# Two gate rows of a modulation: summed by 32-column ones products and spread by DMA instead of by full-width ones products

## The chip, the core and the metric

The kernel runs on 1 core of one Trainium2 chip. The metric is the device time of one execution in microseconds (us); the median of several executions is compared. Engines are named as the profile names them: PE (TensorE), PEld (its weight load), DVE (VectorE), ACT (ScalarE), POOL (GpSimd), SP (SyncE, which here only issues DMAs).

## The reference, cut to what matters

Two transformer blocks on 256 rows of width 1024, all in f32. In the first block a conditioning vector `c` gives six rows of 1024 numbers, two of which are the gates:

```python
mod = jax.nn.silu(c) @ w_ada[l] + b_ada[l]
sh1, sc1, gt1, sh2, sc2, gt2 = jnp.split(mod[:, None, :], 6, axis=-1)
h = modulate(rmsnorm(x, g_norm1[l]), sh1, sc1)        # h * (1 + scale) + shift
...
x_new = x + gt1 * o                                    # o: attention and retention, through w_out
x_new = x_new + gt2 * conv_ffn(modulate(rmsnorm(x_new, g_norm2[l]), sh2, sc2),
                               w_up[l], conv_w[l], conv_b[l], w_down[l])
```

`gt1` and `gt2` multiply all 256 rows, so on the chip each must stand on all 128 partitions, 1024 columns wide. The second block (windowed attention, a gated recurrence, cross attention, a gated feed-forward) does not use the modulation.

## The kernel before, in words

Every large product is made of f32 matrices that are split in a high and a low part (`split_from`, L159, and `Weights.unit`, L217): ACT casts the high part (L223, or L230 with a gain), DVE subtracts to get the low part (L226, L231), and PE adds three products (`mm3`, L180, matmuls at L186). Weights come in 512 KB pieces into five `raw` buffers (L199), loaded by SP's queue (L211, L213). So a piece goes DMA, ACT, DVE, PE, and its `raw` buffer is free for SP's next load when ACT and DVE have read it.

The order of instructions on each engine is not written out: a scheduler behind the tile pools sets it from the program, each engine then works strictly in that order, and buffers of a pool go round. Pools that matter here: PSUM `tr` (2 buffers, L110) and `acc` (4), SBUF `s4` (128x1024, 9 buffers, L293) and `s1k` (128x256, 4 buffers, L295). In the traces `s` stands for a tile of the pool s1, `s4` tiles among them.

The modulation rows of groups 2 to 5 (gt1, sh2, sc2, gt2) are not made on PE alone. `tick` (L517) loads one 128x1024 piece of `w_ada` and DVE adds `silu(c)` times it to an accumulator of its group (L526, L529). With the eighth piece of a group `ada_done` (L496) is called: the accumulator has to be summed over its 128 partitions, which a product with a matrix of ones does. For the gates the full 128-column ones matrix leaves the sum on all 128 partitions at once (L502), in two halves of 512 columns, and DVE adds each half from PSUM to the bias row that already stands on all partitions (L504). For shift and scale only 32 columns of ones are used, four times 256 columns side by side in one PSUM tile (L507, L508), then `ada_fm` (L337) turns the rows.

Ticks fall into these loops: one per unit in the loop over the first 544 columns of `w_in` (L589 to L599), so group 2 is complete at its end; three per unit in strand D (L601), two in E and eight in F (L854, L855), so group 5 ends in the interleaved part that `WEAVE` (L30) writes out, beside attention (`mla_half`, L711) and retention (`retention`, L765). Right behind the loop at L589 stand the query part (L614 to L623), the key part (L639 to L653) with its transposes (L168), the query projection (`w_uq`, L660 to L683) with the rotation (`rope32`, L625; its last step is L636), and a copy inside SBUF by two DMAs from SP (L657). The first user of gt1 is `seg1` (L920), the first of gt2 is `seg2` (L1320), both far behind.

Of the kernel before, what the change touches and what calls it, by code (L numbers as in the profile page):

```python
# [14 lines left out]
ALU = mybir.AluOpType  # L15
# [3 lines left out]
P = 128  # L19
# [70 lines left out]
def _body(nc, tc, A, out, es):  # L90
# [18 lines left out]
    def tr_tile():  # L109
        return ps.tile([P, 512], F32, tag="tr", name="tr", bufs=2)  # L110
# [20 lines left out]
    ones = cp.tile([P, P], F32, name="ones")  # L131
# [156 lines left out]
    with ExitStack() as e1:  # L288
# [4 lines left out]
        S4 = lambda shape=(P, 1024), dt=F32: s.tile(list(shape), dt, tag="s4", name="s4", bufs=9)  # L293
# [11 lines left out]
        for b in range(2):  # L305
            c = slice(b * 512, (b + 1) * 512)
# [25 lines left out]
        def ada_rows(acc):  # L332
            rows = S1()
            nc.scalar.copy(rows, acc[:, 0:256])
            return rows

        def ada_fm(acc, bias, dst, ns=1):  # L337
            rows = ada_rows(acc)
            t = tr_tile()
            for b in range(2):  # L340
                nc.tensor.transpose(t[:, b * P:(b + 1) * P], rows[:, b * P:(b + 1) * P], ident)
            tv = t[:, 0:256].rearrange("p (b q n) -> p n q b", b=2, q=4)
            for i in range(ns):
                nc.vector.tensor_tensor(out=dst[:, 8 * i:8 * i + 8].rearrange("p (q b) -> p q b", b=2), in0=tv[:, i, :, :],
                                        in1=FM(bias).rearrange("p (q b) -> p q b", b=2), op=ALU.add)

        def scale_gain(dst, sc, gname):
            nc.vector.scalar_tensor_tensor(out=dst, in0=sc, scalar=1.0, in1=FM(gname), op0=ALU.add, op1=ALU.mult)
# [145 lines left out]
        bc_row(gt2, "b_gt2")  # L494

        def ada_done(g, acc):  # L496
            if g in (2, 5):
                dst = gt1 if g == 2 else gt2
                for i in range(2):
                    t = tr_tile()  # L500
                    ac = slice(i * 512, (i + 1) * 512)
                    nc.tensor.matmul(t, lhsT=ones, rhs=acc[:, ac], start=True, stop=True)  # L502
                    d = dst[:, i * 512:(i + 1) * 512]
                    nc.vector.tensor_tensor(out=d, in0=d, in1=t, op=ALU.add)  # L504
            else:
                t = tr_tile()
                for q in range(4):  # L507
                    nc.tensor.matmul(t[32 * q:32 * q + 32, 0:256], lhsT=ones[:, 0:32],  # L508
                                     rhs=acc[:, q * 256:(q + 1) * 256], start=True, stop=True)
                ada_fm(t, "b_sh2" if g == 3 else "b_sc2", B2 if g == 3 else A2)  # L510
            if g == 4:
                scale_gain(A2, A2, "g_norm2")
# [4 lines left out]
        def tick(n=1):  # L517
            for _ in range(n):
                if not ada_queue:
                    return  # L520
                g, k = ada_queue.pop(0)
                raw = W().raw()
                nc.sync.dma_start(raw, A["w_ada"][k * P:(k + 1) * P, g * 1024:(g + 1) * 1024])
                if k == 0:
                    ada_cur[g] = S4()
                    nc.vector.tensor_scalar(out=ada_cur[g], in0=raw, scalar1=silc[:, k, 0:1], scalar2=None,  # L526
                                            op0=ALU.mult)
                else:
                    nc.vector.scalar_tensor_tensor(out=ada_cur[g], in0=raw, scalar=silc[:, k, 0:1],  # L529
                                                   in1=ada_cur[g], op0=ALU.mult, op1=ALU.add)  # L530
                if k == 7:
                    ada_done(g, ada_cur[g])
# [871 lines left out]
    for g in range(1, 6):  # L1404
        nb = 4 if g < 5 else 2
        sg = G4()
        for part, mk, us in ((0, tr_tile, ones_w2["gate"][g]), (1, at_tile, ones_w2["up"][g])):
# [3 lines left out]
            for i in range(nb // 2):  # L1411
                c = slice(i * 512, (i + 1) * 512)
                if part == 0:
                    nc.vector.tensor_tensor(out=sg[:, c].rearrange("p (j n) -> p j n", j=2),
                                            in0=accs[i].rearrange("p (j n) -> p j n", j=2),
                                            in1=rbc.unsqueeze(1).broadcast_to([P, 2, T]), op=ALU.mult)
# [99 lines left out]
```

## Time and profile before

| | before |
|---|---|
| median of 3 runs | 854.78 us (853.59 to 857.85) |
| span of the profiled execution | 852.4 us, 12981 instructions |
| PE busy | 822.0 us (96%) |
| DVE busy | 575.9 us (68%) |
| ACT busy | 464.1 us (54%) |
| mean granted TensorE clock | 0.996 of full speed |
| DMA | 154.22 MB, mean 181 GB/s |

The span runs from the first to the last instruction of the profiled execution. A device time of that one execution by itself is not among the numbers; the median of the runs is 2.4 us above the span, and that difference stands for what lies around it.

A row of the timeline gives the start, the duration of one group, the engine, the line, the operation, output<-inputs, the shape and the count; in square brackets stands the idle time of that engine before it and what ended it. [...] "To landing" is the time from a DMA's issue to its last byte with its completion.

### The profile page before, as it was taken

The numbers are of one execution on the slowest core, as the hardware profiler recorded it, in microseconds if no ns is written. First come the engines' busy times: TensorE is split into PE (matmuls) and PEld (weight loads), VectorE is DVE, ScalarE is ACT, GpSimd is POOL, SyncE is SP. The second block draws the span as 40 slices with busy tenths as digits, with TensorE's granted clock in tenths as the row PEclk, the third lists the DMA queues.
The fourth block names the chain that finished last, engine by engine and source line by source line (L and its number), as shares of the span: only waits on it lengthen the run. The fifth ranks groups of instructions, "written<-read, shape, count | busy, mean of one in ns | idle before, by whom it ended". The sixth has DMA issues, their size and how long they took to land.

```text
span 852.4 us, 12981 instructions
## 1 busy us (share of the span) xinstructions
PE 822.0 (96%) x4978; PEld 689.9 (81%) x4978; DVE 575.9 (68%) x881; ACT 464.1 (54%) x749; POOL 53.0 (6%) x91
## 2 busy tenths in 40 slices
PE   6999989999999999999999999999999999999996
PEld 5767976666787898998997877777888899998995
DVE  4339778995787697667577767776847855655642
ACT  6739264234566675555455757665626845554631
POOL 1100020110010000000002200101001100000000
PEclk9999999999999999999999999999999999999999
DMA  8898787863155566666664543443624676666511
GB/s 287 306 316 276 225 257 245 286 228 119 50 161 170 180 219 194 177 191 182 183 188 148 166 144 112 130 141 124 194 78 126 191 227 186 186 186 185 174 50 50
DMA packets 65150, 154.22 MB, mean 181 GB/s; under 512 B 5184, under 2 KB 10816, under 8 KB 65088
## 3 DMA queue, kind: packets, MB, share of 16 engines
q1 hardware_dynamic: 65088, 153.39, 57.6%
q8 instruction: 39, 0.64, 0.3%
q14 instruction: 23, 0.19, 0.1%
HBM read 151.80 MB, written 1.05 MB: 179 GB/s over the span
## 4 chain that ended last, share of the span: by engine, by line
PE 66%; ACT 4%; DVE 3%; issue 1%; POOL 1%; DVEq 0%; POOLq 0%; ACTq 0%
PE acc L186 32%; PE tr L256 12%; PE at L256 12%; PE tr L168 1%; PE at L1280 1%; PE at L1258 1%; PE tr L1199 1%; ACT xh L223 1%; DVE xl L226 1%; ACT junk L144 1%; PE at L1149 1%; PE at L1151 1%; PE tr L742 0%; PE at L771 0%; PE at L788 0%
## 5 line engine op out<-in xcount | busy, mean ns | idle before, releaser
L223 ACT CAST wh<-raw 128x1024 fp32r<-128x1024 f32 (+1 forms) x90 | 91.2, 1015 | 105.9 <-PE acc L186 28.1
L226 DVE TENSOR_TENSOR wl<-raw,wh 128x1024 fp32r<-128x1024 f32 (+1 forms) x87 | 102.3, 1177 | 49.1 <-ACT wh L223 48.1
L226 DVE TENSOR_TENSOR xl<-raw,xh 128x1024 fp32r<-128x1024 f32 x68 | 84.4, 1245 | 43.9 <-ACT xh L223 43.6
L186 PE MATMUL acc<-wh,xTh 128*128 128x512 f32 (+2 forms) x272 | 100.4, 395 | 1.7 <-ACT wh L223 1.4
L223 ACT CAST xh<-raw 128x1024 fp32r<-128x1024 f32 x68 | 71.0, 1049 | 55.9 <-PE tr L256 24.6
L186 PE MATMUL acc<-wl,xTh 128*128 128x512 f32 (+2 forms) x272 | 97.3, 383 | 0.5 <-DVE wl L226 0.5
L186 PE MATMUL acc<-wh,xTl 128*128 128x512 f32 (+2 forms) x272 | 97.5, 383 | 0.0
L231 DVE SCALAR_TENSOR_TENSOR wl<-raw,fm,wh 128x512 fp32r<-128x512 f32 (+3 forms) x96 | 67.3, 744 | 44.4 <-ACT wh L230 43.8
L230 ACT ACTIVATE wh<-raw,fm 128x512 fp32r<-128x512 f32 (+3 forms) x96 | 63.8, 713 | 38.2 <-issue 16.7
L186 PEld LDWEIGHTS acc<-wh,xTh 128*128 128x128 f32 x272 | 50.4, 189 | 13.6 <-issue 2.4
L186 PEld LDWEIGHTS acc<-wl,xTh 128*128 128x128 f32 x272 | 50.5, 189 | 11.7 <-issue 2.3
L186 PEld LDWEIGHTS acc<-wh,xTl 128*128 128x128 f32 x272 | 50.5, 189 | 9.7 <-issue 1.0
L186 PE MATMUL acc<-xh,xTl 128*128 128x512 f32 x144 | 53.5, 397 | 0.0
L186 PE MATMUL acc<-xl,xTh 128*128 128x512 f32 x144 | 53.3, 396 | 0.2 <-DVE xl L226 0.2
L186 PE MATMUL acc<-xh,xTh 128*128 128x512 f32 x144 | 53.2, 397 | 0.0
L186 PE MATMUL acc<-xh,g 128*128 128x512 f32 x160 | 45.6, 397 | 0.0
L231 DVE SCALAR_TENSOR_TENSOR xl<-raw,fm,xh 128x512 fp32r<-128x512 f32 (+1 forms) x44 | 33.3, 796 | 17.8 <-ACT xh L230 17.7
L230 ACT ACTIVATE xh<-raw,fm 128x512 fp32r<-128x512 f32 (+1 forms) x44 | 31.2, 757 | 22.4 <-issue 12.9
L529 DVE SCALAR_TENSOR_TENSOR s<-raw,silc,s 128x1024 f32<-128x1024 f32 x28 | 39.0, 1393 | 6.2 <-DMA raw<-in_w_ada_dram 6.1
L186 PE MATMUL acc<-wh,g 128*128 128x512 f32 x128 | 37.1, 397 | 0.0
L186 PEld LDWEIGHTS acc<-xh,g 128*128 128x128 f32 x160 | 29.7, 189 | 6.7
L186 PEld LDWEIGHTS acc<-xl,xTh 128*128 128x128 f32 x144 | 26.7, 188 | 6.4 <-DVE xl L226 1.1
(373 smaller groups left out, 1745.1 us busy)
## 6 DMA issues: line engine op xcount, KB each, us to landing
raw<-in_w_up_dram SPq DMA_DIRECT2D x66, 512.0 KB, 3.8
raw<-in_w_ada_dram SPq DMA_DIRECT2D x48, 512.0 KB, 5.5
raw<-in_w_down_dram SPq DMA_DIRECT2D x44, 512.0 KB, 3.6
raw<-in_w_in_dram SPq DMA_DIRECT2D x38, 512.0 KB, 3.9
raw<-in_w_gate_dram SPq DMA_DIRECT2D x22, 512.0 KB, 4.1
raw<-in_w_out_dram SPq DMA_DIRECT2D x16, 512.0 KB, 3.6
raw<-in_wk_x_dram SPq DMA_DIRECT2D x8, 512.0 KB, 6.7
raw<-in_wv_x_dram SPq DMA_DIRECT2D x8, 512.0 KB, 5.7
```

The lines of the kernel that those rows point to most:

```text
L144: nc.scalar.activation(junk[:, 0:a.shape[-1]], a, AF.Square, scale=n ** -0.5, accum_out=ss)
L168: nc.tensor.transpose(t[:, j * P:(j + 1) * P], src[:, (b + j) * P:(b + j + 1) * P], ident)
L186: nc.tensor.matmul(accs[i], lhsT=xl if f == 2 else xh, rhs=wl[i] if f == 1 else wh[i], start=first and f == 0, stop=last and f == 2)
L223: nc.scalar.copy(wh[:, 0:n], raw[:, 0:n])
L226: eng.tensor_tensor(out=wl[:, 0:n], in0=raw[:, 0:n], in1=wh[:, 0:n].bitcast(F32), op=ALU.subtract)
L230: nc.scalar.activation(wh[:, s], raw[:, s], AF.Copy, scale=gains[k])
L231: nc.vector.scalar_tensor_tensor(out=wl[:, s], in0=raw[:, s], scalar=gains[k], in1=wh[:, s].bitcast(F32), op0=ALU.mult, op1=ALU.subtract)
L256: nc.tensor.matmul(accs[b // 2][:, (b % 2) * T:(b % 2 + 1) * T], lhsT=wt[:, o:o + P], rhs=xt[:, k, :], start=k == 0 and fl == 0 and b % 2 ...
L529: nc.vector.scalar_tensor_tensor(out=ada_cur[g], in0=raw, scalar=silc[:, k, 0:1], in1=ada_cur[g], op0=ALU.mult, op1=ALU.add)
L1149: nc.tensor.matmul(o[cs, hs], lhsT=ATs[cs, cols], rhs=ih[cs, hs], start=True, stop=cg == 0)
L1151: nc.tensor.matmul(o[cs, hs], lhsT=qi[:, cols], rhs=Sst[cg - 1][:, hs], start=False, stop=True)
L1199: nc.tensor.matmul(sc[:, j * nk:(j + 1) * nk], lhsT=qTs[pr_, hd * P:(hd + 1) * P], rhs=kTs[pr_, 0:nk], start=True, stop=True)
```

## The change

All four groups are now summed by the 32-column products, which leave column block q of the sum on partitions 32q to 32q+31. For the gates ACT copies them from PSUM to an `s1k` tile (`ada_rows`, L332), and four DMAs on ACT's own queue each read one row of 256 numbers (1 KB) from partition 0, 32, 64 or 96 and write it to all 128 partitions of a new `s4` tile (128 KB each). One DVE instruction of 128x1024 adds that tile to the bias row.

```diff
         def ada_done(g, acc):
+            t = tr_tile()
+            for q in range(4):
+                nc.tensor.matmul(t[32 * q:32 * q + 32, 0:256], lhsT=ones[:, 0:32],
+                                 rhs=acc[:, q * 256:(q + 1) * 256], start=True, stop=True)
             if g in (2, 5):
+                gt = S4()
                 dst = gt1 if g == 2 else gt2
-                for i in range(2):
-                    t = tr_tile()
-                    ac = slice(i * 512, (i + 1) * 512)
-                    nc.tensor.matmul(t, lhsT=ones, rhs=acc[:, ac], start=True, stop=True)
-                    d = dst[:, i * 512:(i + 1) * 512]
-                    nc.vector.tensor_tensor(out=d, in0=d, in1=t, op=ALU.add)
+                rows = ada_rows(t)
+                for q in range(4):
+                    c = slice(q * 256, (q + 1) * 256)
+                    nc.scalar.dma_start(gt[:, c], rows[32 * q:32 * q + 1, :].unsqueeze(1).broadcast_to([1, P, 256]))
+                nc.vector.tensor_tensor(out=dst, in0=dst, in1=gt, op=ALU.add)
             else:
-                t = tr_tile()
-                for q in range(4):
-                    nc.tensor.matmul(t[32 * q:32 * q + 32, 0:256], lhsT=ones[:, 0:32],
-                                     rhs=acc[:, q * 256:(q + 1) * 256], start=True, stop=True)
                 ada_fm(t, "b_sh2" if g == 3 else "b_sc2", B2 if g == 3 else A2)
```

The number of lines stays the same; in the changed kernel the products are L499, the DMAs L507 and the DVE addition L508.

The scheduler also places other instructions anew. In the rows below, `waits` lists the counters an instruction waits on: an engine's name, or DMAHW for the completion counters of DMAs (a number after the underscore only belongs to the name).

**Place 1** is the end of the loop at L589, where group 2 (gt1) is completed. On ACT before, between the two `w_uq` casts (L230) and the cast of strand D's first weight piece (L223), the query copies (L616) and sums of squares (L144) stand:

```order
L230 ACTIVATE wh<-raw,fm 128x768
L616 COPY s1k<-acc 128x256
L144 ACTIVATE junk,ss_1177<-acc 128x256
L230 ACTIVATE wh<-raw,fm 128x768
L616 COPY s1k<-acc 128x256
L144 ACTIVATE junk,ss_1189<-acc 128x256
L223 CAST wh<-raw 128x1024
```

On ACT with the change:

```order
L230 ACTIVATE wh<-raw,fm 128x768 x2
L223 CAST wh<-raw 128x1024
L334 COPY s1k<-tr 128x256
L616 COPY s1k<-acc 128x256
L507 DMA s_1168<-s1k 128x1x256 x4
L144 ACTIVATE junk,ss_1184<-acc 128x256
L160 CAST s_1176<-tr 128x2x128
L616 COPY s1k<-acc 128x256
```

The cast L223 has moved ahead of both query copies; the gate's copy and its four DMAs stand behind the first of them.

On DVE at the same place before, with the two gate additions (L504) and the query part's subtractions (L161) behind them:

```order
L504 TENSOR_TENSOR bc<-bc,tr 128x512 [waits PE_49]
L226 TENSOR_TENSOR wl<-raw,wh 128x1024 [waits DMAHW4_49,Activation_49]
L504 TENSOR_TENSOR bc<-bc,tr 128x512 [waits PE_49]
L161 TENSOR_TENSOR s_1170<-tr,s_1169 128x2x128 [waits Activation_49]
L630 TENSOR_TENSOR s1k<-acc,c_92 128x32
L634 TENSOR_TENSOR s1k<-acc,c_92 128x2x8 x2
L161 TENSOR_TENSOR s_1170<-tr,s_1169 128x2x128 [waits Activation_49]
```

On DVE with the change:

```order
L161 TENSOR_TENSOR s_1177<-tr,s_1176 128x2x128 [waits Activation_49]
L508 TENSOR_TENSOR bc<-bc,s_1168 128x1024 [waits DMAHW2_49,DMAHW3_49,DMAHW1_49,DMAHW0_49]
L161 TENSOR_TENSOR s_1177<-tr,s_1176 128x2x128 [waits Activation_49]
L630 TENSOR_TENSOR s1k<-acc,c_92 128x32 [waits Activation_49]
L634 TENSOR_TENSOR s1k<-acc,c_92 128x2x8 x2
L636 TENSOR_TENSOR kpe<-s1k 128x32 [waits DVE_49]
L231 SCALAR_TENSOR_TENSOR wl<-raw,fm,wh 128x1024 [waits DMAHW4_49,Activation_49]
L161 TENSOR_TENSOR s_1179<-tr,s_1178 128x2x128 [waits Activation_49] x2
L630 TENSOR_TENSOR s1k<-acc,c_92 128x32
L634 TENSOR_TENSOR s1k<-acc,c_92 128x2x8 [waits DVE_49]
L634 TENSOR_TENSOR s1k<-acc,c_92 128x2x8
L526 TENSOR_SCALAR s_1341<-raw,silc 128x1024 [waits DMAHW5_49]
```

The addition L508 stands behind the first L161 and waits for all four DMAs; one L231 has moved ahead of the key part's L161.

**Place 2** is where group 5 (gt2) is completed, in retention. On ACT with the change, from the gate's copy (L334) to the exponentials of two heads (L777, L778), with the state copy of a head (L774) between:

```order
L334 COPY s1k<-tr 128x256
L774 COPY s1k<-at 128x256
L507 DMA s_2184<-s1k 128x1x256 [waits Activation_49]
L507 DMA s_2184<-s1k 128x1x256 x2
L507 DMA s_2184<-s1k 128x1x256 [waits DMAHW4_49]
L777 ACTIVATE s1k<-s_1488,lg 128x256
L778 ACTIVATE s1k<-s_1488,lg 128x256
L782 ACTIVATE s_2244<-s_1488,nlb 128x384
L223 CAST xh<-raw 128x1024 [waits DMAHW6_49]
L774 COPY s1k<-at 128x256 [waits DVE_49,PE_49]
L777 ACTIVATE s1k<-s_1488,lg 128x256 [waits DMAHW3_49,DMAHW4_49,DMAHW2_49,DMAHW1_49]
```

Before, no DMA stood on ACT's queue; now the second head's L777, which takes the `s1k` buffer that the gate's DMAs read, waits for all four.

On DVE at place 2 before:

```order
L161 TENSOR_TENSOR xTl<-tr,xTh 128x4x128
L504 TENSOR_TENSOR bc<-bc,tr 128x512
L805 BN_STATS bn_2207<-acc 128x6
L783 SCALAR_TENSOR_TENSOR s_2230<-s_1481,lg,s_2230 128x384
L504 TENSOR_TENSOR bc<-bc,tr 128x512
L806 BN_AGGR rmv_1483<-bn_2207 128x2
L805 BN_STATS bn_2214<-acc 128x6
L226 TENSOR_TENSOR xl<-raw,xh 128x1024
L806 BN_AGGR rmv_1484<-bn_2214 128x2
L779 TENSOR_TENSOR s1k<-s1k,s_818 128x256
```

On DVE at place 2 with the change:

```order
L779 TENSOR_TENSOR s1k<-s1k,s_818 128x256 [waits Activation_49]
L780 TENSOR_TENSOR s1k<-s1k,s_818 128x256 [waits Activation_49]
L783 SCALAR_TENSOR_TENSOR s_2244<-s_1488,lg,s_2244 128x384 [waits Activation_49]
L508 TENSOR_TENSOR bc<-bc,s_2184 128x1024 [waits DMAHW3_49,DMAHW4_49,DMAHW2_49,DMAHW1_49]
L805 BN_STATS bn_2221<-acc 128x6 [waits PE_49]
L805 BN_STATS bn_2228<-acc 128x6 [waits PE_49]
L806 BN_AGGR rmv_1490<-bn_2221 128x2 [waits DVE_49]
L779 TENSOR_TENSOR s1k<-s1k,s_818 128x256 [waits Activation_49]
```

The addition stands between the last step of one head and the first products' factors (L779) of the next, and waits for the four DMAs.

## Rows read from the trace of the kernel before

**Rows 1.** The page, part 4: the chain that ended last, by engine.

```profile
PE 66%; ACT 4%; DVE 3%; issue 1%; POOL 1%; DVEq 0%; POOLq 0%; ACTq 0%
```

**Rows 2.** The timeline of PE from 106 to 131 us.

```profile
110.92 1.88 PE L502 MATMUL tr<-s,ones 128*128 128x512 f32 x4
...
115.21 0.92 PE L186 MATMUL acc<-wh,xTh 128*128 128x512 f32 x2 [1.38 <-ACT wh L223]
...
130.84 1.08 PE L681 MATMUL tr<-ident,s 128*96 128x128 f32 x8 [2.00 <-DVE s L636]
```

**Rows 3.** The timeline of ACT from 110 to 116 us.

```profile
110.08 0.35 ACT L616 COPY s1k<-acc 128x256 f32<-128x256 f32 x1
...
114.11 1.05 ACT L223 CAST wh<-raw 128x1024 fp32r<-128x1024 f32 x1 [1.85 <-DMA raw<-in_w_in_dram]
```

**Rows 4.** The timeline of DVE from 122 to 131 us.

```profile
122.72 0.75 DVE L161 TENSOR_TENSOR s<-tr,s 128x256 fp32r<-128x256 f32 x2
...
124.58 1.29 DVE L231 SCALAR_TENSOR_TENSOR wl<-raw,fm,wh 128x1024 fp32r<-128x1024 f32 x1
...
129.16 1.28 DVE L529 SCALAR_TENSOR_TENSOR s<-raw,silc,s 128x1024 f32<-128x1024 f32 x1 [2.56 <-DMA raw<-in_w_ada_dram]
130.36 0.42 DVE L636 TENSOR_TENSOR s<-s1k 128x256 f32<-128x256 f32 x1
```

**Rows 5.** DVE's busy time in one stretch, with granted clock, DMA share and GB/s.

```profile
118.29:122.72 4.43, 3.95 (x16) 0.92 0.40 114
```

**Rows 6.** The timeline of SP's DMA issues at 122.8 us.

```profile
122.84 0.33 SPq L523 DMA_DIRECT2D raw<-in_w_ada_dram  x1
```

**Rows 7.** The instructions of line L657: issue ns (min/median/max), and time to landing.

```profile
L657 SPq DMA_DIRECT2D s<-s x2: 593/669/745, 125.1 to 125.9; - x2
...
DMA to landing us min/median/max: 6.3/6.5/6.8
```

**Rows 8.** DMA issues: count, KB each, median us to landing.

```profile
raw<-in_w_up_dram SPq DMA_DIRECT2D x66, 512.0 KB, 3.8
...
out_dram<-xr SPq DMA_DIRECT2D x4, 256.0 KB, 2.0
```

**Rows 9.** Stretches of 1 us: PE, PEld, DVE, ACT, POOL, PEclk, DMA share, GB/s.

```profile
115.00:116.00 1.00, 0.79 (x2) 0.30 (x2) 0.81 (x1) 0.92 (x5) 0.38 (x1) 0.80 0.93 381
117.00:118.00 1.00, 1.00 (x4) 0.63 (x3) 0.07 (x2) 0.82 (x3) 0.83 (x3) 0.50 0.92 135
128.00:129.00 1.00, 0.83 (x5) 0.51 (x3) 0.00 (x0) 1.00 (x2) 0.00 (x0) 1.00 1.05 190
```

**Rows 10.** The chain that ended last, 222 to 240 us: start, us, what.

```profile
228.04 0.22 PE acc L801 x2
...
229.50 1.05 PE tr L502 x2
...
231.45 0.86 PE tr L502 x2
...
232.53 0.89 PE at L771 x8
233.43 0.86 PE at L788 x4
...
237.23 1.85 PE acc L186 x8
```

**Rows 11.** The timeline of PE at 190 us, the sums of group 4.

```profile
190.12 0.64 PE L508 MATMUL tr<-s,ones 128*32 128x256 f32 x8
```

**Rows 12.** The timeline of ACT at 225 us.

```profile
225.53 0.37 ACT L774 COPY s1k<-at 128x256 f32<-128x256 f32 x1 [0.95 <-PE at L771]
```

**Rows 13.** The timeline of DVE from 237 to 241 us.

```profile
237.83 0.49 DVE L805 BATCH_NORM_STATS2 bn<-acc 128x6 f32<-128x128 f32 x2
...
240.87 0.43 DVE L779 TENSOR_TENSOR s1k<-s1k,s 128x256 f32<-128x256 f32 x1 [0.16 <-ACT s1k L777]
```

**Rows 14.** The page, part 5: DVE with two SBUF inputs of 128x1024.

```profile
L226 DVE TENSOR_TENSOR xl<-raw,xh 128x1024 fp32r<-128x1024 f32 x68 | 84.4, 1245 | 43.9 <-ACT xh L223 43.6
```

## Prediction, made before the changed kernel was run

> **What bounds the kernel now.** The page's chain of waits comes first: two thirds of the span end on PE [rows 1], so a product left out saves its time only where PE was not about to wait anyway. I therefore read the timelines of all engines at the two places where a gate row is summed, then the DMA rows for what a spread could cost. 0.5%, about what a measurement of this kernel can tell from no change, is 4.3 us.
>
> At place 1 (gt1) PE does wait. Behind the gate products (1.88 us for both halves) stand 1.38 us of idle time that ended with ACT's cast L223, and at 130.84 another 2.00 us that ended with DVE's L636 [rows 2]. The cast itself had waited 1.85 us for its weights [rows 3], and DVE before L636 had waited 2.56 us for a `w_ada` piece [rows 4]. The reader is to see a ring here: SP issues that piece at 122.84 [rows 6], because at 122.72 DVE has worked through the pieces before it; it lands at 129.16, 6.3 us later; L529 (1.28) and L636 (0.42) follow, and then PE. Whatever delays DVE before 122.7 delays the load too.
>
> At place 2 (gt2) PE runs through, and both gate halves, 1.05 and 0.86 us, lie on the chain [rows 10].
>
> **Savings.** The 32-column products cost 0.64 us per group, as those of group 4 do [rows 11]. At place 1 the 1.24 us saved lie ahead of a wait of 1.38 us whose end a DMA sets: counted as nothing, and if that cover were gone at most 1.2 us. At place 2: 1.05 + 0.86 - 0.64 = 1.27 us, on the path, all counted. DVE's addition now has two SBUF inputs, 1.24 us of 128x1024 [rows 14]; the two that it replaces are off the path, so in itself it counts as nothing.
>
> **Additions on ACT.** One copy of 128x256, 0.35 to 0.37 us [rows 3, 12], and four issues. ACT has issued no DMA; the nearest rows are SP's, 0.33 us for a plain load [rows 6] and 0.67 us (0.59 to 0.75) for the copies inside SBUF [rows 7]. I take 0.67, four in 2.7 us, since those have the same kind of source. The copies and issues themselves hold up no product that isn't also behind the addition.
>
> **The four landings** decide. DVE's L508 waits for all four, and the trace shows no DMA that reads one partition. Lower bound 2.0 us, the landing of 256 KB from SBUF to the output; between stand 3.8 us for a weight piece [rows 8] and 6.5 us for the two copies of L657, which read 32 partitions [rows 7]. For the upper bound I compare rates. At 128 to 129 us, with these copies under way, the DMA engines are busy at a share of 1.05 and yet move only 190 GB/s; at 115 to 116, with weights from DRAM, 381 GB/s at 0.93 [rows 9], which is 381 / (0.93 x 16) = 25.6 GB/s for one engine. So a read from few partitions is served at half the rate with every engine occupied. Here each DMA reads a single partition 128 times over. If all engines together get from it no more than the 25.6 GB/s that one engine moves elsewhere, 128 KB take 5.1 us, and the four, one behind another on one queue, 20.5 us: with the fixed 2.0 us the last lands 22.5 us after the first issue. I take this value: going from DRAM to 32 partitions halved the rate, and one partition is 32 times further in the same direction.
>
> **Place 1 by that.** ACT has moved the cast L223 ahead; with the landing of its weights at 114.11 and 1.05 us it ends at 115.16 [rows 3]. Two copies of 0.35 end at 115.8, where the issues begin. The last landing S is 115.8 + 2.0 + 20.5 = 138.3. Behind L508 on DVE stand, in order, its own 1.24 us, the work that filled 3.95 us of 118.29 to 122.72 [rows 5], the L231 moved ahead (1.29) and two L161 (0.75 together) [rows 4]: 7.2 us. Only then is the `raw` buffer free, SP issues the next `w_ada` load, 3.8 us in a quiet queue [rows 8], and 1.28 + 0.42 lead to PE's L681 [rows 4]. Sum: S + 12.7 = 151.0 against 130.84 [rows 2], so **+20.2 us**. SP's later loads wait on the same buffers and start no earlier; gt1's user is far behind, so it is the place in DVE's order that costs, not the need for the row. ACT is held too, since the second key copy takes the `s1k` buffer that the DMAs read.
>
> **Place 2 by that.** The sums start at 229.50 [rows 10] and end at 230.15; two copies of 0.37 [rows 12] end at 230.9. The last landing is 230.9 + 22.5 = 253.4. Behind it DVE needs 1.24, a statistic of 0.49 and L779's 0.43 [rows 13, 14] for the next head's factors: 255.6. PE has until then, in the changed order, 12 products of L186 (1.85 / 8 = 0.23 each), eight of L771 (two groups of 0.89), two of L788 (0.86) and eight pairs of 0.22 [rows 10], 7.2 us, to 237.3. It stands for 18.3 us. After an idle time the granted clock falls: it is 0.50 at 117 to 118 [rows 9], behind the 1.38 us of waiting at 115.21 [rows 2], against 1.00 at 128 to 129 [rows 9]. For the restart I count three microseconds at that lower level, 1.5 us lost (an estimate). Place 2: 18.3 + 1.5 - 1.27 = **+18.5 us**.
>
> **Sum.** 852.4 + 20.2 + 18.5 = 891.1 us of span; the median of the runs lies 2.4 us above the span, so 893.5, **893 us**.
>
> **Rivals.**
> *Two reads at a time* (chance 0.16). [...]
>
> *An ordinary landing* (0.17). The source doesn't matter and the last lands 3.8 to 6.5 us after its issue at 118.5 (115.8 + 2.7). With 6.5: S = 125.0, +6.9; place 2 ready at 242.3, 5.0 + 1.5 - 1.27 = +5.2; +12.1, 867 us. With 3.8: +4.2 and +1.0, 860 us. For it: L657's landings are measured with both copies sharing the engines.
>
> *The shortest landing* (0.12): 2.0 us. S = 120.5, +2.4 at place 1; at place 2 the stall is 0.5, so -0.8. 854.0 + 2.4 = 856 us, within 0.5%. For it: only the output rows. [...]
>
> *Faster* (0.06). The rows land before DVE reaches L508, within 1 us or so of the copy. Then DVE at place 1 is free earlier, by the addition moved off PSUM and PE's shorter sums, the fourth `w_ada` load starts up to 2 us earlier, and PE's 2.00 and 1.38 us vanish with the 1.27: -4.65, 850 us. It decides at a landing below some 1 us, and the smallest in the rows is 2.0.
>
> **How the numbers follow.** The forecast has 0.49. Its upper end: reading 8% slower (190 GB/s is 11.9 an engine, and half of 25.6 is 12.8), 1.6 us at each of two places, and the fourth load landing in 6.3 instead of 3.8, +2.5: 893.5 + 5.7, 899 to 900. The range reaches down over the second and third cases to 860; left out are the shortest landing and the gain, 0.18, and a tail of 0.02. So 860 to 900. Faster by over 0.5%: 0.06; within 0.5%: 0.12; slower: 0.49 + 0.16 + 0.17 = 0.82.
>
> **What would show it.** In the changed profile: L507's landing around 20 us at the last of four; DVE idle before L508 at both places, ended by a DMA; a stretch of full DMA share with little moved, 30 to 60 GB/s; PE idle for some 20 us from before L681 and some 18 before the next head's L800, ended by DVE, and a clock of 0.50 behind each; the rest of the span unchanged. A landing near 5 us gives the third case, near 10 the second. Wrong altogether would be DVE coming to L508 after the landing, or PE having more independent work at place 2 than the order shows.

## The result, and the profile after

| | before | with the change |
|---|---|---|
| median | 854.18 us (850.53 to 857.85, 6 runs) | 887.73 us (884.58 to 888.92, 6 runs) |
| ratio | | 1.0375, 95% interval 1.0351 to 1.0399 |
| profiled execution | span 852.4 us | 884.58 us, span 882.8 us |

The kernel became 33.5 us slower. The forecast was 893 us, in a range of 860 to 900. The profiled execution of the changed kernel is the shortest of its six.

The chain that ended last, by engine, is first to be read against [rows 1]. DMA, which had no share in it, now has 2%:

```profile
PE 63%; ACT 4%; DVE 3%; DMA 2%; POOL 1%; issue 1%; ACTq 0%; DVEq 0%; POOLq 0%
```

The instructions of L507, the eight new DMAs, with the nanoseconds of an issue (minimum, median, maximum), who waited for them, and their time to landing:

```profile
L507 ACTq DMA_DIRECT2D s<-s1k x8: 477/1516/5325, 112.1 to 247.1; - x8
...
  DVE bc L508: 17.2, 2
  ACT s1k L777: 8.3, 1
  ACT s1k L643: 3.7, 1
...
DMA to landing us min/median/max: 7.1/12.9/15.7
```

That is counted for each DMA from its own issue. From the first issue to the moment when DVE starts L508 it is 130.82 - 112.08 = 18.7 us at place 1 and 262.89 - 243.49 = 19.4 us at place 2, as DVE's timeline shows:

```profile
130.82 1.23 DVE L508 TENSOR_TENSOR bc<-bc,s 128x1024 f32<-128x1024 f32 x1 [8.34 <-DMA s<-s1k]
...
262.89 1.23 DVE L508 TENSOR_TENSOR bc<-bc,s 128x1024 f32<-128x1024 f32 x1 [8.90 <-DMA s<-s1k]
```

The timeline of ACT shows a second wait at each place. The four issues occupy ACT for 9.16 and 8.39 us, and the instruction behind them counts that time as "issue"; then the next user of the copy's `s1k` buffer waits for the DMAs:

```profile
112.08 9.16 ACTq L507 DMA_DIRECT2D s<-s1k  x4
121.29 0.38 ACT L144 ACTIVATE junk<-acc 128x256 bf16<-128x256 f32 x1 [8.96 <-issue]
...
130.81 0.47 ACT L643 ACTIVATE s1k<-acc,rs 128x256 f32<-128x256 f32 x1 [3.71 <-DMA s<-s1k]
...
243.49 8.39 ACTq L507 DMA_DIRECT2D s<-s1k  x4
251.92 0.51 ACT L777 ACTIVATE s1k<-s,lg 128x256 f32<-128x256 f32 x1 [8.19 <-issue]
...
262.87 0.51 ACT L777 ACTIVATE s1k<-s,lg 128x256 f32<-128x256 f32 x1 [8.30 <-DMA s<-s1k]
```

PE stands twice at each place, first behind ACT's issues, then behind DVE's addition. The row of L681 answers to the one at 130.84 in [rows 2]:

```profile
121.82 0.80 PE L186 MATMUL acc<-wh,xTh 128*128 128x512 f32 x1 [9.00 <-ACT junk L144]
...
132.70 0.80 PE L186 MATMUL acc<-wh,xTh 128*128 128x512 f32 x1 [5.54 <-DVE s1k L634]
...
143.98 1.03 PE L681 MATMUL tr<-ident,s 128*96 128x128 f32 x8
...
252.94 1.22 PE L800 MATMUL acc<-s1k 128*128 128x128 f32 x4 [5.65 <-DVE s1k L779]
...
264.97 1.22 PE L800 MATMUL acc<-s1k 128*128 128x128 f32 x4 [5.76 <-DVE s1k L779]
```

How long the landing takes is explained by four stretches (columns as in [rows 9]: a stretch, its length, the busy time and count of PE, PEld, DVE, ACT and POOL, the granted clock as a share of full speed, the busy share of the 16 DMA engines and the GB/s that they moved):

```profile
116.00:119.00 3.00, 0.00 (x0) 0.00 (x0) 0.00 (x0) 0.00 (x0) 0.00 (x0) 0.50 0.85 31
...
247.00:262.00 15.00, 6.56 (x28) 5.74 (x26) 1.44 (x3) 2.65 (x5) 0.00 (x0) 0.77 0.78 30
...
253.00:258.00 5.00, 5.00 (x22) 4.90 (x23) 0.90 (x2) 1.58 (x3) 0.00 (x0) 0.50 0.83 36
...
265.00:269.00 4.00, 4.00 (x18) 3.91 (x19) 2.63 (x8) 2.84 (x7) 0.00 (x0) 0.50 0.14 19
```

At 116 to 119 the DMA engines are busy at a share of 0.85 and move 31 GB/s; in [rows 9] a share of 0.93 moved 381. The last two rows show the price behind a stall: PE works all the time, at a granted clock of 0.50, for 5.00 and 4.00 us.

**Where the time went.** SP issues the first `w_uq` load before any engine has come to an instruction that the change moved. The first row is of before, the second of the changed kernel:

```profile
105.62 1.16 SPq L211 DMA_DIRECT2D raw<-in_w_uq_dram  x2
...
103.97 1.30 SPq L211 DMA_DIRECT2D raw<-in_w_uq_dram  x2
```

So this execution was 1.65 us ahead before the change could act. L681 starts 143.98 - 130.84 = 13.1 us later, so place 1 cost 13.1 + 1.65 = 14.8 us. The span is 30.4 us longer, so what comes behind it cost 30.4 - 13.1 = 17.3 us. That is place 2 alone: at PE's first L926, behind retention, the distance is 300.0 - 269.5 = 30.5 us already, and it stays so to the end.

### The profile page after: what moved, and what is told of

Same layout as the page of the kernel before. It is cut to its first block, busy times and chain, and to the rows that moved or that the text cites. A ratio compares the mean times of both kernels' runs of the same rounds, so it can differ in the third digit from the quotient of the medians.

```text
span 882.8 us, 13020 instructions
## 1 busy us (share of the span) xinstructions
PE 827.9 (94%) x4986; PEld 695.3 (79%) x4986; DVE 575.8 (65%) x879; ACT 464.6 (53%) x751; POOL 53.5 (6%) x91
## 3 DMA queue, kind: packets, MB, share of 16 engines
q10 hardware_dynamic: 1152, 1.05, 2.6%
## 4 chain that ended last, share of the span: by engine, by line
PE 63%; ACT 4%; DVE 3%; DMA 2%; POOL 1%; issue 1%; ACTq 0%; DVEq 0%; POOLq 0%
PE acc L186 30%; PE tr L256 12%; PE at L256 12%; DMA s<-s1k 2%; PE tr L168 1%; DVE xl L226 1%; PE at L1280 1%; PE at L1258 1%; PE tr L1199 1%; ACT xh L223 1%; ACT junk L144 1%; PE at L1149 0%; PE at L1151 0%; ACTq L507 0%; PE at L1229 0%
## 5 line engine op out<-in xcount | busy, mean ns | idle before, releaser
L223 ACT CAST wh<-raw 128x1024 fp32r<-128x1024 f32 (+1 forms) x90 | 91.0, 1012 | 101.1 <-PE acc L186 29.6
L186 PE MATMUL acc<-wh,xTh 128*128 128x512 f32 (+2 forms) x272 | 101.6, 399 | 15.7 <-ACT junk L144 9.0
L223 ACT CAST xh<-raw 128x1024 fp32r<-128x1024 f32 x68 | 70.8, 1046 | 55.4 <-PE tr L256 24.6
L231 DVE SCALAR_TENSOR_TENSOR wl<-raw,fm,wh 128x512 fp32r<-128x512 f32 (+3 forms) x96 | 67.2, 743 | 42.6 <-ACT wh L230 42.0
L230 ACT ACTIVATE wh<-raw,fm 128x512 fp32r<-128x512 f32 (+3 forms) x96 | 63.7, 712 | 35.9 <-issue 16.8
L231 DVE SCALAR_TENSOR_TENSOR xl<-raw,fm,xh 128x512 fp32r<-128x512 f32 (+1 forms) x44 | 33.3, 797 | 17.8 <-ACT xh L230 17.8
L230 ACT ACTIVATE xh<-raw,fm 128x512 fp32r<-128x512 f32 (+1 forms) x44 | 31.2, 756 | 22.5 <-issue 13.0
L529 DVE SCALAR_TENSOR_TENSOR s<-raw,silc,s 128x1024 f32<-128x1024 f32 x28 | 38.8, 1387 | 2.8 <-DMA raw<-in_w_ada_dram 2.7
```

The source lines that it names most:

```text
L186: nc.tensor.matmul(accs[i], lhsT=xl if f == 2 else xh, rhs=wl[i] if f == 1 else wh[i], start=first and f == 0, stop=last and f == 2)
L223: nc.scalar.copy(wh[:, 0:n], raw[:, 0:n])
L230: nc.scalar.activation(wh[:, s], raw[:, s], AF.Copy, scale=gains[k])
L231: nc.vector.scalar_tensor_tensor(out=wl[:, s], in0=raw[:, s], scalar=gains[k], in1=wh[:, s].bitcast(F32), op0=ALU.mult, op1=ALU.subtract)
```

## The experiments

Theory 1 at the start: a DMA that reads one partition 128 times is slow, and what stands in order behind its landing and its issue waits. First its core, the read.

### Which partitions are read (src32, src4_near, src4_far)

```diff
-nc.scalar.dma_start(gt[:, c], rows[32*q:32*q + 1, :].unsqueeze(1).broadcast_to([1, P, 256]))
+nc.scalar.dma_start(gt[:, c], rows[32*q:32*q + 32, :].unsqueeze(1).broadcast_to([32, 4, 256]))    # src32
+nc.scalar.dma_start(gt[:, c], rows[32*q:32*q + 4, :].unsqueeze(1).broadcast_to([4, 32, 256]))     # src4_near
+nc.scalar.dma_start(gt[:, c], rows[32*q:32*q + 32:8, :].unsqueeze(1).broadcast_to([4, 32, 256]))  # src4_far
```

All 32 partitions of a block hold the same row, so the result is the same.

src32:

> Each of the eight DMAs still writes 128 KB to 128 partitions, but reads 32 partitions of the gate's copy (all 32 hold the same row) four times each instead of one partition 128 times; the order on every engine is that of the changed kernel. Theory 1 (a read of one partition is slow, 31 GB/s in the changed kernel's trace, and everything queued behind the four landings and the four issues waits for it): the four DMAs of a place land within some 5 us (512 KB at the 190 GB/s that the copies from 32 partitions reached is 2.8 us, and 2 fixed) instead of 18.7 and 19.4, ACT's third and fourth issue fall from 2.4 to 5.3 us to about 0.6, and the time to 854 to 859 us. Theory 2 (the cost is the number of small packets, 128 of 1 KB per DMA, wherever they are read): landings, issues and time stay as in the changed kernel, 884 to 889 us. Theory 3 (the wait in DVE's and ACT's order costs whatever the landing is): landing short, but still 865 us or more.

src4_near:

> Each DMA reads four neighbouring partitions (32q to 32q+3), 32 times each; order on the engines unchanged. If each partition by itself limits the read, four give 4 x 31 = 124 GB/s: 512 KB in 4.2 us, the last landing about 6 to 7 us after the first issue, and the time is 855 to 862 us. If neighbouring partitions are read through one common port that gives 31 GB/s, nothing changes: last landing 19 us, time 884 to 889 us.

src4_far:

> Each DMA reads four partitions eight apart (32q, 32q+8, 32q+16, 32q+24), 32 times each; order on the engines unchanged. By both theories of the run before (a limit per partition, or per port of neighbouring partitions) this gives four times the rate of one: last landing 6 to 7 us after the first issue, 855 to 862 us. Only if the number of packets counts does it stay at 884 to 889 us.

| DMA reads | time, us | ratio to before (95%) | first issue to L508, place 1 |
|---|---|---|---|
| one partition (the change) | 887.7 | 1.0375 (1.0351 to 1.0399) | 18.7 us |
| 4 neighbouring | 894.1 | 1.0464 (1.0426 to 1.0501) | 136.28 - 115.14 = 21.1 us |
| 4, eight apart | 869.2 | 1.0173 (1.0137 to 1.021) | 125.61 - 113.96 = 11.7 us |
| 32 | 858.3 | 1.0049 (1.003 to 1.0068) | 121.36 - 113.95 = 7.4 us |

The line of the gate's DMAs in part 3 of the page gives packets, MB and the share of 16 engines' span that the packets took, here for the change, src4_near, src4_far and src32:

```profile
q10 hardware_dynamic: 1152, 1.05, 2.6%
...
q10 hardware_dynamic: 1056, 1.05, 0.9%
...
q10 hardware_dynamic: 1056, 1.05, 0.4%
...
q10 hardware_dynamic: 1152, 1.05, 0.4%
```

Theory 2, that the number of packets costs the time, falls: src32 has the 1152 packets of the change. So does theory 3, that the wait costs whatever the landing is: with the same order on every engine, the read from 32 partitions takes back 29 of the 33 us. In src32 the issues fall to some 0.6 us each, and the landing of each DMA to 3.7 to 5.7 us:

```profile
L507 ACTq DMA_DIRECT2D s<-s1k x8: 551/630/642, 114.0 to 234.7; - x8
...
DMA to landing us min/median/max: 3.7/4.8/5.7
```

The last landing came 7.4 us behind the first issue at place 1, where weight loads were under way (335 GB/s in all at 116 to 120 us), and 5.7 at place 2; some 5 were expected.

The two runs with four partitions differ in nothing but which four. The first row is of src4_near, while its DMAs run without much else, the second of src4_far:

```profile
120.00:136.00 16.00, 5.19 (x16) 3.80 (x16) 0.42 (x1) 4.85 (x16) 3.92 (x10) 0.61 0.20 31
```

```profile
119.00:125.00 6.00, 5.02 (x15) 3.46 (x13) 0.00 (x0) 3.17 (x10) 2.95 (x8) 0.61 0.26 88
```

Four neighbours give 31 GB/s, no more than one partition; four that lie eight apart give 88. So what limits the read here isn't one partition's own: one alone got 31 GB/s (116 to 119 us of the change), four neighbours together 31 and 25 at the two places, four eight apart 88.

src4_near, at 894.1 us, missed its 884 to 889: from the first issue to L508 it takes 21.1 and 23.1 us at the two places, against 18.7 and 19.4 with one partition. At place 2 only 25 GB/s were moved (256 to 271 us). Why it is slower than one partition was not tested.

The expectation of four times 31 GB/s for src4_far was too high, and with it that of 855 to 862 us. The DMA share shows why: 0.26, about 4 of the 16 engines, against 0.85 with one partition. By that share (an estimate) some four engines do the work, and 88 / (0.26 x 16) = 21 GB/s each is not far below the 25.6 that an engine moved in [rows 9]; in src4_near the shares are 0.20 and 0.22, 3.2 and 3.5 of the 16 engines. The packets of src4_far took no more engine time in all than those of src32 (0.4% each), so its read isn't slow any more; what differs is the share, 0.26 in src4_far and 0.92 in src32 (116 to 120 us, with weight loads).

### One place at a time (only_gt1, only_gt2)

```diff
-            if g in (2, 5):
+            if g in (2,):          # only_gt1; (5,) in only_gt2; the other gate as in the kernel before
```

> The change at gt1 alone; gt2 is summed by the two full-width products as before. From the traces place 1 came out 13.1 us later (PE's L681 at 143.98 against 130.84) and the rest of the span 17.3 us, so the theory of two separate stalls expects about 867 us (864 to 870). The rival, that one place's stall covers the other's (loads that were late anyway), expects the larger part at one place: below 860 or above 875 us.

> The change at gt2 alone; gt1 as before. By the traces place 2 cost 17.3 us, so 871 us (868 to 874); with the 870.0 us of the run with gt1 alone the two would then give 854 + 16 + 17 = 887, the changed kernel's time, and the stalls are separate. Clearly less or more than that means that one place changes what the other costs.

870.0 us (ratio 1.0186, 1.0149 to 1.0222) and 872.1 us (1.0213, 1.0165 to 1.0261): 16.0 and 17.4 us above the runs of before beside them, as expected. Their sum is 33.4, and the change cost 33.5: the two stalls are separate.

### Who is held (add_pool, bf_act1, bf_pool1)

Three things may hold PE: DVE's wait for the landing, ACT's hold in the issues, and loads that stand behind the slow reads in the DMA engines. add_pool moves the issues to POOL's queue and keeps the addition. The two others (bias first) add the bias before the spread, into a tile of their own, so that no engine waits for the landing:

```diff
-                rows = ada_rows(t)
+                rows = gr                          # a 128x256 tile of its own
+                for q in range(4):
+                    b = slice(32 * q, 32 * q + 32)
+                    nc.vector.tensor_tensor(out=rows[b, :], in0=gt[b, q*256:(q+1)*256], in1=t[b, 0:256], op=ALU.add)
...
-                nc.vector.tensor_tensor(out=dst, in0=dst, in1=gt, op=ALU.add)
```

Here `gt` is the gate's own tile, and the DMAs write into it, from ACT's queue (bf_act1) or POOL's (bf_pool1). The scheduler places other instructions anew in all three, so they are less clean than the runs above.

> The eight DMAs, still reading one partition each, are issued from POOL's queue; DVE's addition still waits for them. ACT is no longer held by the issues (9.2 us at place 1, 8.4 at place 2 in the changed kernel). If the landing that DVE waits for sets the end, nothing is won: the last landing stays 17 to 20 us after the first issue, time 880 to 892 us. If ACT's hold was the stall, the time falls by most of the 9.0 and 5.7 us that PE spent waiting behind it: 868 to 875 us.

> The bias is added before the spread (four DVE additions of 32x256 from PSUM), into a 128x256 tile of its own, and the DMAs from ACT's queue write straight into the gate's tile: no engine waits for the landing, which only the gates' users far behind need. The reads are still of one partition, so ACT is still held by its third and fourth issue, 8 to 9 us at each place. Theory: of the +33 us only what ACT's hold costs is left: at place 1 up to 9.0 less the 3.4 us that PE idled there before, at place 2 up to 5.7 less the 1.3 saved, so 854 + (0 to 9) + (0 to 5): 858 to 868 us. The rival, that the slow transfers cost by themselves (they fill the 16 DMA engines for 17 us and hold up the weight loads): 870 us or more.

> As the run before, with the DMAs on POOL's queue: neither DVE nor ACT waits for the issues or the landing, and the reads are still of one partition. If in-order waiting behind the slow reads is the whole cost, it is gone: 852 to 857 us, no change against the kernel before. If the slow reads also cost by filling the DMA engines ahead of the weight loads, 858 us or more: in the changed kernel the w_ukv load issued beside them needed up to 11.6 us to land instead of some 4.

**add_pool**: 884.4 us (1.0354, 1.0271 to 1.0437). DVE waits longer than in the changed kernel, 12.5 and 16.0 us, with ACT free. ACT's hold is not needed for the stall:

```profile
136.51 1.23 DVE L508 TENSOR_TENSOR bc<-bc,s 128x1024 f32<-128x1024 f32 x1 [12.50 <-DMA s<-s1k]
...
267.56 1.23 DVE L508 TENSOR_TENSOR bc<-bc,s 128x1024 f32<-128x1024 f32 x1 [16.03 <-DMA s<-s1k]
```

**bf_act1**: 870.6 us (1.0198, 1.015 to 1.0246), 16 us above before. That is above the 858 to 868 expected of ACT's hold alone, and just inside what was given to the rival, that the slow transfers cost by themselves (870 or more). No DVE instruction waits for the rows now, and the hold is there as it was (groups of waits: engine, line, what it waited for, us, times, longest):

```profile
ACT s L160 <- issue: 9.0, 1, 9.0
```

**bf_pool1**: 878.3 us (1.0283, 1.0241 to 1.0325). Expected were 852 to 857, and here theory 1 as it stood fell: nothing waits for the gate's landing, ACT issues nothing, and it is 23.7 us slower. The waits of ACT at place 1 and place 2 name the cause:

```profile
ACT wh L230 <- DMA raw<-in_w_ukv_dram: 9.7, 1, 9.7
...
ACT xh L223 <- DMA raw<-in_w_out_dram: 11.7, 1, 11.7
```

These are weight loads, issued by SP beside the reads. The two `w_ukv` loads landed 8.4 and 19.3 us after their issue, where the kernel before needed 3.5 to 6.4 for its loads of that line:

```profile
DMA to landing us min/median/max: 8.4/13.9/19.3
```

The second of them was issued at 117.9, so it is under way in all of this stretch of bf_pool1, where all DMAs together move 33 GB/s at a share of 0.80:

```profile
120.00:125.00 5.00, 5.00 (x18) 4.21 (x18) 2.90 (x13) 3.25 (x8) 0.99 (x3) 0.50 0.80 33
```

So a third way is open to the stall: the slow reads occupy the DMA engines, and what is loaded beside them is late.

### The read mended, and nobody waiting (bf_act32, bf_pool32)

```diff
-rows[32*q:32*q + 1, :].unsqueeze(1).broadcast_to([1, P, 256])
+rows[32*q:32*q + 32, :].unsqueeze(1).broadcast_to([32, 4, 256])
```

> The bias added before the spread as in the two runs before, DMAs from ACT's queue, each reading 32 partitions four times. Theory as it stands: what the change costs is three things that all come from the slow read (DVE's wait for the landing, ACT's hold in the third and fourth issue, and weight loads that stand behind the reads in the DMA engines: 9.7 us for w_ukv and 11.7 us for w_out in the run on POOL's queue). With 32 partitions the reads are done in some 3 us, ACT issues in 0.6 us each, and no engine waits for the landing: 851 to 856 us, no change against the kernel before, and below the 858.3 us of the run that kept DVE's addition behind the landing. The rival, that any DMA placed at these two points costs through the loads behind it: 857 us or more.

> As the run beside it, from POOL's queue; the order of DVE, PE and ACT is that of the POOL run with one partition, so the two differ in the read alone. If the crowding of the DMA engines by the slow reads made that run 878 us, this one falls to 851 to 856 us, with waits of ACT for w_ukv and w_out of under 3 us. If POOL's way of issuing (its share of the DMA queues, or its place) was the cause, it stays above 865 us.

855.0 us (1.002, 1.0002 to 1.0038) and 856.4 us (1.0032, 1.0018 to 1.0045); the second lies 0.4 us above the 851 to 856 expected. bf_pool32 has the order of bf_pool1 on every engine, and the read alone takes back 22 us of 24; its `w_ukv` loads land in about 5 us:

```profile
DMA to landing us min/median/max: 4.7/5.1/5.4
```

bf_act32 is the best form of the change that was tried, and no faster than the kernel before. The 1.27 us that PE saves at place 2 are not seen in the time. Against src32, which keeps DVE's addition behind the landing, it is 3.3 us faster by the medians, but the intervals of the two ratios overlap.

## Why the prediction was right, point by point

**The read of one partition** was the step that carried the forecast, and it held. The rate was 31 GB/s, not the 25.6 taken from one engine's rate, so the four landings took 18.7 and 19.4 us, not 22.5. They came one behind another, as the forecast had them: 7.7, 11.7, 16.3 and 18.6 us after the first issue at place 1. That a landing has a fixed part of 2.0 us, the output rows' whole landing, was the author's estimate; no run splits a landing in two. That the rate came so near is partly luck: that all engines together get no more than one engine's rate was an assumption, and what the runs show is 31 GB/s from one partition, 25 to 31 from four neighbours and 88 from four that lie eight apart. The step from the 190 GB/s of L657 to a slow read was also bolder than it looked: these copies write only 32 partitions too, and the row does not say which side held them. src32 fills that gap: its DMAs read 32 partitions and write the same 128 as the change, and each lands 3.7 to 5.7 us after its issue instead of 7.1 to 15.7; at 233 to 238.5 us all DMAs together move 191 GB/s at a share of 0.67.

**Place 1**: +20.2 forecast, +14.8 measured. The landing gives -3.8. The issues began 2.1 us earlier than forecast (112.08 + 1.65 = 113.7 against 115.8), for the most part because the weights of the moved cast L223 landed 4.5 us after their issue, where the forecast took the 6.4 of the trace of before. From L508 to L681 it was 143.98 - 130.82 = 13.2 us instead of 12.7, +0.5. Together -5.4. The ring through DVE, the `raw` buffer and the next load is there, and its size came out: SP issues that load 6.6 us behind L508 (7.2 forecast), and it lands in 4.2 (3.8):

```profile
137.44 0.33 SPq L523 DMA_DIRECT2D raw<-in_w_ada_dram  x1
...
141.92 1.28 DVE L529 SCALAR_TENSOR_TENSOR s<-raw,silc,s 128x1024 f32<-128x1024 f32 x1
143.12 0.42 DVE L636 TENSOR_TENSOR s<-s1k 128x256 f32<-128x256 f32 x1
```

But at its end nothing waits any more: L529 stands behind DVE's own work, and L681 behind products that PE had put off. That both ways end within half a microsecond of each other is luck.

**Place 2**: +18.5 forecast, +17.3 measured, with two errors against each other. (The products that PE still had to do were sixteen of L771 and four of L788; the times that the forecast counts for them are right.) The landing was 3.1 us shorter. But PE had its work cut off earlier, since the first head's L777 stands behind the issues on ACT, and the clock stayed at 0.50 for longer than three microseconds, at 253 to 258 and again at 265 to 269; three is what the trace of before shows, at 116 to 119 us. That the clock falls after an idle time held behind all four stalls here (0.50 also at 122 to 125 and 133 to 136 us), but not behind the 2.00 us before L681 in [rows 2], where it stays at 1.00 from 119 to 140 us. So the forecast's sign, PE idle for some 20 and 18 us on end, did not come: PE idles 9.00 and 5.54 us at place 1 and 5.65 and 5.76 at place 2, and the rest of the cost, part of it work at the lower clock, was not split up further.

**The mis-sized term is the cost of the issues**: "four in 2.7 us". They took 9.16 and 8.39 us, and "hold up no product that isn't also behind the addition" was wrong as a description: PE stood 9.00 us behind ACT alone. The sum did not suffer, because the landing ended still later, and with ACT free (add_pool) the kernel is no faster; bf_act1 shows what ACT's hold, with the crowding of the loads, costs when nothing waits for the landing, 16 us.

**SP's loads.** The forecast looked at when they start, and not at when those already issued land. That is the second gap, and bf_pool1 shows its size, 23.7 us where nothing else is left. In the changed kernel no instruction on ACT waits for a `w_ukv` load, whose two landings take 5.3 and 11.6 us: the waits on DVE and ACT cover it, so the three do not add.

**The total**: the profiled execution, 884.6 us, lies 8.9 below 893.5, from -5.4 (place 1), -1.2 (place 2), the 1.65 us that it was ahead, and 0.6 in the time around the span (884.58 - 882.8 = 1.8, against 2.4). The median is 5.8 below.

**The rivals.** Two reads at a time would have halved the 20.5 us and put the last landing near 12; it came at 18.7, with the four one behind another. No run shows which of the partitions 0, 32, 64 and 96 can be read side by side. The ordinary landing did not happen, but it is what src32 measures, 858.3 us, just below what that rival gave (860 to 867; the sum for 860 leaves out the 1.5 us of the restart at place 2, which the one for 867 has). The gain needed a landing under 1 us; the shortest of these DMAs in any run took 2.6 us, in the bias-first kernels with 32 partitions.

**What stays open.** bf_act1 is 8 us faster than bf_pool1 although ACT is held in it. Its issues are spread over 9 us, which may let weight loads in between (its `w_ukv` loads landed after 5.1 and 13.2 us). But the order differs too, and POOL's queue moves the same rows in a third of the packets, here in bf_pool1, against the 1152 of ACT's queue:

```profile
q0 software_dynamic: 384, 1.05, 3.0%
```

The three weren't told apart.

## What to carry to other kernels

Where a row is to go to all partitions and copies of it stand on many already, as behind the 32-column ones product here, try reading many that lie apart: reading all 32 instead of one took the cost from 33 us to 4 (887.7 and 858.3 us), without moving an instruction. Four neighbouring ones won nothing (894.1), four eight apart a part (869.2). Look in the profile for a high DMA share with few GB/s (0.85 with 31 GB/s in the change; with four neighbouring source partitions the share was low too, 0.20), and then ask three questions: who waits for the landing, who is held in the issue, and which loads are queued behind. Mending one or two of the three left the rest here (add_pool 884.4, bf_act1 870.6, bf_pool1 878.3 us); mending the read mended all (bf_act32 855.0).

## What the runs showed of the hardware that was not expected

- An issue can hold its engine: in the changed kernel the third L507 took 2.4 to 2.6 us and the fourth 4.8 to 5.3, against 0.5 to 0.6 for the first two. The same four issues took 2.6 us together in src32, where the reads were fast. On POOL's queue (add_pool) they took 2.2 to 2.5 us even with the slow reads.
- The share of busy DMA engines went with the shape of the read: with four source partitions it was 0.20 to 0.26, with one 0.71 to 0.85, with 32 it was 0.67 (src32, 233 to 238.5 us, all DMAs together).
- Slow reads delay other DMAs by far more than their 0.5 MB suggest: a 512 KB weight load beside them landed after up to 19.3 us (bf_pool1), against 4.7 to 5.4 in bf_pool32 with the mended read.
